# Issuing the column groups of a modulation block together, in a two-layer hybrid diffusion kernel on one core

## The chip, the core and the metric

The kernel runs on one core of a Trainium2 chip. The metric is device time in microseconds of one execution. The engines are called as in the profile: PE multiplies matrices (PEld loads its weights), DVE, ACT and POOL are the vector, scalar and GpSimd engines, SP issues most DMA transfers. Each engine works through its own instructions in order, and they wait for each other through semaphores.

## The reference, cut to what matters

Two layers run over 256 context and 512 latent tokens with 1024 channels. Each layer takes six vectors (shift, scale and gate, twice) from a modulation product:

```
mod_l = silu(c)     @ mod_w[i] + mod_b[i]     # 6144 columns, latent stream
mod_c = silu(c_ctx) @ mod_w[i] + mod_b[i]     # the same weights, context stream
sh1, sc1, g1, sh2, sc2, g2 = split(mod, 6)
p = (norm(x) * (1 + sc1) + sh1) @ w_in[i]     # first modulation: shift, scale
y = concat(gmlp(p), attention(p), deltanet(p))
x = layer_norm(a * x + g1 * (y @ w_out[i]))   # gate
x = layer_norm(a * x + g2 * mlp(norm(x) * (1 + sc2) + sh2))
```

The attention has six query heads on two key and value heads. The DeltaNet is a gated recurrence over chunks of 64 tokens, for six heads, forward and backward.

## The kernel before, in words

**Tiling.** Tokens lie in six tiles of 128 (two of context, four latent). Most products are made in fp32, or with the operands split into a high and a low part.

**The modulation products of layer 0.** The 6144 columns are taken as three products of 2048 columns: 0 (first shift and scale), 1 (first gate and second shift) and 2 (second scale; the second gate is summed elsewhere). The left operand has 32 columns, two of which are used, so a 512-column group of the product fills one quarter of the rows of an output tile: `pm[32*g : 32*g+32]` for group g. The contraction has `KD` = 8 blocks of 128 channels. Product 0 is `mod_in` (line 451), at the kernel's start: two halves, each 8 blocks of two groups. Product 1 is `mod(0, 1, 4, ...)`: 8 blocks of four groups, 32 matmuls. Product 2 is `mod(0, 2, 2, ...)`: 8 blocks of two groups, 16 matmuls. Each matmul has its own weight tile `modw` (128x512 fp32, 256 KB) from DRAM. In `mod` (line 388) there are four such buffers and one bias tile `modb`: four loads go out ahead, then each step waits in the plan for one tile, issues one matmul and one load. At the end DVE adds the bias (`modb<-mm,modb`), PE transposes the result (`mm<-c_ident,modb`), DVE copies shift or scale, and the gate rows go to DRAM (`gates_d<-modb`).

**The stage they run in.** `mods()` (line 856) is one of several streams that run beside each other (line 887): the scans and operands of three DeltaNet head pairs (`scans`, `makes`: rows of the trace with `S`, `vn`, `rr`, `rT`, `rK`, `rQ`, `rW`, `rA`, `gs`), the preparation of the third pair (`prep(2)`: inverses, `PA`, `PB`, `M`), and the attention by tile and head (`akh`, `akl`, `qs`, `ape`, `apT`, `ava`). The pairs 0 and 1 are scanned first, pair 2 after them. A latent attention head is four score matmuls `akh`, `akl`, with the transposes `c_ident,ape` and products `ava,apT` of the head before.

**What sets the order.** The order is made twice. The class `Flow` interleaves the streams while the program is traced: it keeps a rough cost of each instruction (`cost`, line 74) and goes on with the stream whose last step ends first; a stream can give a key or a time that it waits for. `BIAS` and `AHEAD` put some streams ahead. A scheduler then orders each engine's instructions by its own estimate of their times. Instructions that were traced one behind the other may so stand apart.

All instructions are issued by one helper, so every row of the trace has line L206.

**The last piece that the change touches** is `z_gate` (line 1017): the gate of the DeltaNet's output of token tile t, made by `vz` (line 825) after the projections.

Of the kernel before, what the change touches and what calls it, by code (L numbers as in the profile page):

```python
# [39 lines left out]
class Flow:  # L40
    """Interleaves streams of work (generators that yield after each step) as they are traced. The engines run what is
    traced in order, so the stream whose last step ends first, by a rough cost of each instruction, goes on next. A stream
    yields a generator to start it, a key to wait until that key is in `done`, a tuple of classes of PSUM tiles to get,
    or the time to go on."""

    # wait for a result of the same engine, of another one
# [14 lines left out]
    def lend(self, cls, tiles):  # L61
        """PSUM tiles for the streams to ask for"""
        self.spare[cls] = [(0.0, i) for i in range(len(tiles))]
        for i, t in enumerate(tiles):
            self.slots[cls, i] = t
# [8 lines left out]
    def cost(self, eng, op, out, ins, kw):  # L74
        n = max([self.width(out)] + [self.width(a) for a in ins])
        if eng == "tensor":
            n, m = self.width(out), out.shape[0]
            if op == "transpose":
                return 0.87 * n
            if ins[-1].dtype == F32R:  # L80
                return max(35.0 + 0.56 * m, 0.42 * n)
            return 2.0 * max(35.0 + 0.62 * m, 0.83 * n)
# [32 lines left out]
    def when(self, s):  # L115
        """the time a stream can go on, None while what it waits for is not there"""
        t, w = s[0], s[3]
        if isinstance(w, str):
            return max(t, self.done[w]) if w in self.done else None
        if w:  # L120
            for cls in set(w):
                k = w.count(cls)
                if len(self.spare[cls]) < k:
                    return None
                t = max(t, sorted(self.spare[cls])[k - 1][0])
        return t

    def run(self, *gens, side=(), drain=False):
        """until the streams gens end; those of side go on in the next run if they have not ended, or else with drain"""
# [37 lines left out]
    def step(self, gen, val, ahead):  # L167
        """one step of a stream, its instructions as if they were traced that much earlier"""
# [8 lines left out]
    def aside(self, gen):  # L177
        """starts a stream that need not end with the run"""
        self.start(gen, self.last, False)

    def start(self, gen, now, main, bias=0.0, ahead=0):
        """a stream, or a list of it with the ns and the instructions it has ahead of others"""
# [5 lines left out]
    def drop(self, ap):  # L188
        """gives a PSUM tile back, after the last instruction on it"""
# [21 lines left out]
class _Core:  # L211
    """the engines, with a note of all that is issued to them"""
# [6 lines left out]
def _tb(v):  # L219
    """token tile whose chunks the backward direction takes at step pair v (the forward one takes tile v)"""  # L220
# [7 lines left out]
class Feed:  # L228
    """units of weights in order: float32 loaded `raw` ahead, at most `parts` of them as float32r parts, after a
    product with scale(i) where it gives one; the loads start after the key hold"""  # L230
# [53 lines left out]
class K:  # L284
# [22 lines left out]
    def setup(self):  # L307
# [29 lines left out]
        # scratch in DRAM  # L337
# [7 lines left out]
    def store(self, out, in_):  # L345
        """a store, traced when the data is about to be there: loads keep a queue to themselves"""
# [6 lines left out]
    def psum(self, *ns):  # L353
        """PSUM tiles of n columns, to be dropped after their last use"""
# [12 lines left out]
    def feed(self, name, side, srcs, raw, parts, scale=None, hold=""):  # L367
        """a pool for weight units with the stream that loads and splits them"""
# [12 lines left out]
    def rsqrt(self, out, in_, n, scale=1.0, eps=EPS):  # L381
        """out = (in_ * scale + eps) ** -0.5 on [P, n]"""
# [5 lines left out]
    def mod(self, l, j, n, wt, bt, bufs):  # L388
        """the first n groups of 512 columns from column j*2048 of the modulation, both streams; pieces of weights in tiles
        wt(), a bias tile from bt()"""  # L390
# [18 lines left out]
        for i in range(n * KD):  # L409
            k, g, w = i // n, i % n, ws.pop(0)  # L410
            yield flow.ready[w.tensor.name][0]
            nc.tensor.matmul(pm[32 * g : 32 * g + 32], self.cz[:, k, :], w, start=(k == 0), stop=(k == KD - 1))
            if i + bufs < n * KD:
                load(i + bufs)
                if i + bufs == n * KD - 1:
                    flow.signal(f"mw{l}{j}")
# [34 lines left out]
    def mod_in(self, wt, bt, bufs):  # L451
        """shift and scale of the first layer's input, one half of the channels after the other"""
# [52 lines left out]
    def mod_dve(self, l, w, ss, wt, at, vt, bufs):  # L505
        """vector w (shift, scale, gate; twice) of the modulation for the streams ss, summed over the channel blocks on the
        vector engine and over the partitions by the tensor engine"""
# [67 lines left out]
    def norm_act(self, out, x, n):  # L575
        """(x - mean) * rstd on the scalar engine"""
# [6 lines left out]
    def modulate(self, l, which, t, xn, xh, xl, vt, ks=(0, 1), share=False):  # L583
        """normalised token tile t: scaled and shifted, to channel-major parts, in the halves ks of the channels; with share
        the vector engine scales some"""
# [32 lines left out]
    def chan(self, unit, xh, xl, rng):  # L618
        """channel-major block: psum [P, tokens] for the token columns of rng"""
# [14 lines left out]
    def tokm(self, units, rows, w, c0, c1, t, xh, xl):  # L634
        """token-major block: psum [P, c1-c0] for token tile t; units[i] holds the k-rows rows[i], each w wide"""
# [22 lines left out]
# head start of the longest chain over other streams, ns  # L658
BIAS = 1000.0
# instructions the first preparations are ahead for the scheduler  # L660
AHEAD = 300
# units of the hidden layer taken together; more at the end, where the norms follow each tile
# pieces of the first modulation weights loaded ahead
# [3 lines left out]
# channel blocks of each half that the vector engine takes in the first modulation  # L667
# [3 lines left out]
class Kernel(K):  # L671
# [23 lines left out]
    def mix(self, l, xp, xh, xl, rest):  # L695
        """rest: pools of the layer before that its last streams use"""
# [5 lines left out]
        # gMLP: u channel-major, v token-major with the gates of the DeltaNet  # L702
# [75 lines left out]
        # the weights of the next phase come in meanwhile  # L778
# [6 lines left out]
        # DeltaNet: convolutions of all heads, preparation of the first pairs; attention: q, k, v; gate of the DeltaNet  # L785
# [61 lines left out]
        # attention proper beside the scans  # L847
# [94 lines left out]
    def att_tab(self, l, at):  # L942
        """rotary tables times the norm gains: [q|k, cos|sin, tile, channel]"""
# [14 lines left out]
    def qk_norm(self, l, t, h0, ps, at):  # L958
        """rms-norm and rotary of the q|k heads h0.. of token tile t, then channel-major"""
# [57 lines left out]
    def z_gate(self, l, t, ps):  # L1017
        """silu(z) times the gain of the DeltaNet's output norm"""
        nc, ap_ = self.nc, self.atmp
        pz, ps = ps, ps[:, 128:512]  # L1020
        if t == self.tiles[0]:
# [15 lines left out]
    def attention(self, l, at):  # L1037
        """scores of a head run ahead of the products of the head before"""
# [13 lines left out]
        for t in self.tiles:  # L1052
            n = CTX if t < 2 else TOK
            sl = slice(t * P, t * P + P)
            # q as [hi; lo] on the contraction rows, [lo; hi] for odd heads
# [80 lines left out]
    def dn_conv(self, l, u, c0, r, qkv):  # L1136
        """q, k or v of a head pair from its projection r: convolution, silu, norms; token-major"""
# [11 lines left out]
        # outputs run over cb columns a..b  # L1149
# [15 lines left out]
        # acc is twice the silu; to token-major  # L1165
# [11 lines left out]
        else:  # L1177
            # sums of squares over the channels of each head
# [7 lines left out]
            # l2 norm of x = acc / 2 with its guard; q also carries 1/8  # L1186
# [15 lines left out]
    def dn_gates(self, l, gt, gp, dp, G):  # L1202
        """decay sums and rates of all heads, [P, direction, tile, head]"""
# [18 lines left out]
        # softplus(x) = max(x, 0) + log(1 + e^-|x|), the log as 2 atanh(e / (2 + e))  # L1222
# [25 lines left out]
        # running sums of g within a chunk, from the start (gc) and to the end (rem), per direction  # L1248
# [10 lines left out]
        # gc as rows, to be broadcast over partitions through DRAM  # L1259
# [10 lines left out]
        # the rate beta scales columns forward (with k in the state's update), rows backward (with k and v in the solve)  # L1270
# [13 lines left out]
        # decay of a whole chunk on the state's partitions (direction, dk): [ , step pair, e, head]  # L1284
# [13 lines left out]
    # zero quarters of a block-diagonal lhsT [K, v, head, 2 e + column half, 64], by K half  # L1298
# [9 lines left out]
    def a_tiles(self, l, pool, p):  # L1308
        """compact operands of head pair p: products of queries and keys by group, inverses"""
# [16 lines left out]
    def dn_prep(self, l, p, qkv, G, A, TT):  # L1326
        """products of keys and of queries with keys in each chunk of a head pair, and the transposed inverse of the
        unit-triangular system TT [token, (direction, head, tile), token of the chunk]"""
# [19 lines left out]
        # decay between tokens; rows of M hold j forward and i backward  # L1348
# [59 lines left out]
        # inverses of the unit-triangular 32x32 diagonal blocks, one block per partition  # L1408
# [22 lines left out]
        # X[r, c] is the transposed inverse's [c, r]  # L1431
# [6 lines left out]
        # the off-diagonal 32x32 blocks  # L1438
# [33 lines left out]
    def dn_make(self, l, p, v, qkv, G, A, TT, r):  # L1472
        """operands of the two steps of step pair v"""
# [10 lines left out]
        def rows(w, src, sb):  # L1484
            """src scaled by token, forward and backward tiles side by side, to channel-major blocks"""
# [451 lines left out]
```

## Time and profile before

| what | value |
|---|---|
| time, median of three runs | 2101.5 us (2100.75 to 2103.27) |
| profiled execution, span | 2099.3 us |
| what lies around the span (median less span) | 2.2 us |
| mean granted clock of PE | 0.958 |
| PE busy | 1944.5 us, 93% of the span |
| DVE, ACT, POOL busy | 1358.6 (65%), 921.4 (44%), 195.3 us (9%) |
| stage with scans, attention and modulation products of layer 0 | about 302 to 575 us |

The profiled execution has no time of its own beside its span. Most `f32` matmuls have two records in the trace: "x2" is one matmul `mm<-modw,cz` of a product, "x4" are two of them. A row of the time line starts when the instructions do, and idle time in front of it stands in brackets with its releaser. Ends of matmuls are modelled and overlap the next start, so a slot is read from start to start.

### The profile page before, as it was taken

How to read it: one execution, taken by the hardware profiler on the slowest of the kernel's cores; microseconds unless marked ns; L12 is line 12 of the kernel's file. 1: busy time of each engine (PE TensorE's matmuls, PEld its weight loads, DVE VectorE, ACT ScalarE, POOL GpSimd, SP SyncE). 2: the span in 40 equal slices, each digit the busy share in tenths (PEclk: the TensorE clock that was granted, in tenths of full speed). 3: DMA queues.
4: the chain of work that ended last, by engine and by line, in shares of the span. 5: the costliest groups of instructions: out<-in, count | busy, mean ns of one | idle time of the engine just before them, and what ended most of it. 6: DMA issues, size and time to landing. Idle time of an engine off the chain costs nothing. (4 is left out here: it accounts for less than half of the span.)

```text
span 2099.3 us, 31005 instructions
## 1 busy us (share of the span) xinstructions
PE 1944.5 (93%) x11870; PEld 1601.5 (76%) x11870; DVE 1358.6 (65%) x2659; ACT 921.4 (44%) x1881; POOL 195.3 (9%) x375
## 2 busy tenths in 40 slices
PE   6999779989898999999999989997988889999998
PEld 2887655678777888888888778875877768788886
DVE  5578887865577436362457777889896485544555
ACT  4444346566645322322232265443866445422341
POOL 1111221010012000000000111122100010000001
PEclk8999989989999999999999979977999999999999
DMA  7311024312335424241445243110101434322231
GB/s 280 103 46 51 16 75 149 117 40 64 112 110 181 132 72 159 81 140 43 139 161 173 98 142 95 53 36 26 34 23 30 166 129 164 107 90 81 96 107 59
DMA packets 98240, 208.91 MB, mean 100 GB/s; under 512 B 30850, under 2 KB 45058, under 8 KB 98092
## 3 DMA queue, kind: packets, MB, share of 16 engines
q1 hardware_dynamic: 86956, 189.24, 27.9%
q10 hardware_dynamic: 11136, 17.70, 2.2%
q8 instruction: 93, 1.52, 0.3%
q14 instruction: 55, 0.45, 0.1%
HBM read 184.38 MB, written 17.79 MB: 96 GB/s over the span
## 5 line engine op out<-in xcount | busy, mean ns | idle before, releaser
L206 ACT ACTIVATE whi<-wraw 128x1024 fp32r<-128x1024 f32 (+2 forms) x188 | 194.9, 1050 | 440.6 <-PE ax L206 287.8
L206 DVE TENSOR_TENSOR wlo<-wraw,whi 128x1024 fp32r<-128x1024 f32 (+2 forms) x188 | 226.4, 1211 | 224.6 <-ACT whi L206 224.1
L206 PE MATMUL mm<-x2xh,whi 128*128 128x256 f32 (+1 forms) x832 | 288.4, 347 | 10.5 <-ACT whi L206 9.0
L206 PE MATMUL mm<-x2xh,wlo 128*128 128x256 f32 (+1 forms) x832 | 287.3, 346 | 1.6 <-DVE wlo L206 1.6
L206 PE MATMUL mm<-x2xl,whi 128*128 128x256 f32 (+1 forms) x832 | 287.7, 346 | 0.0
L206 PE MATMUL ax<-whi,hh 128*128 128x512 f32 x640 | 251.2, 392 | 0.0
L206 PE MATMUL ax<-whi,hl 128*128 128x512 f32 x640 | 250.0, 391 | 0.0
L206 PE MATMUL ax<-wlo,hh 128*128 128x512 f32 x640 | 249.9, 390 | 0.0
L206 PEld LDWEIGHTS mm<-x2xh,whi 128*128 128x128 f32 x832 | 158.9, 191 | 34.1 <-ACT whi L206 9.4
L206 DVE TENSOR_TENSOR acc<-acc,ax 128x1024 f32<-128x1024 f32 x68 | 82.9, 1219 | 148.3 <-PE ax L206 148.1
L206 PEld LDWEIGHTS mm<-x2xh,wlo 128*128 128x128 f32 x832 | 158.6, 191 | 22.6 <-DVE wlo L206 2.4
L206 PEld LDWEIGHTS mm<-x2xl,whi 128*128 128x128 f32 x832 | 158.8, 191 | 19.9
L206 PEld LDWEIGHTS ax<-whi,hh 128*128 128x128 f32 x640 | 120.2, 188 | 29.7 <-ACT hh L206 5.2
L206 PEld LDWEIGHTS ax<-whi,hl 128*128 128x128 f32 x640 | 120.1, 188 | 27.5 <-DVE hl L206 2.9
L206 PEld LDWEIGHTS ax<-wlo,hh 128*128 128x128 f32 x640 | 120.2, 188 | 27.0 <-issue 2.6
L206 ACT ACTIVATE rl<-mm 128x256 f32<-128x256 f32 (+1 forms) x104 | 50.7, 490 | 129.1 <-PE mm L206 123.7
L206 DVE SCALAR_TENSOR_TENSOR acc<-modw,cz,acc 128x1024 f32<-128x1024 f32 x80 | 101.2, 1280 | 8.4 <-DMA acc<-in_mod_b 5.4
L206 POOL TENSOR_SCALAR rs<-mv 128x1 f32<-128x1 f32 x52 | 33.1, 637 | 699.1 <-DVE mv L206 696.8
L206 PE MATMUL mm<-ava,apT 128*128 128x128 f32 x624 | 88.4, 285 | 2.7 <-ACT apT L206 1.2
L206 PEld LDWEIGHTS mm<-ava,apT 128*128 128x128 f32 x624 | 78.8, 197 | 7.2 <-ACT apT L206 3.2
L206 DVE TENSOR_TENSOR hl<-rl,hh 128x768 fp32r<-128x768 f32 (+2 forms) x76 | 54.4, 716 | 29.4 <-ACT hh L206 29.4
L206 DVE SCALAR_TENSOR_TENSOR cacc<-cb,cw,cacc 128x772 f32<-128x772 f32 (+1 forms) x72 | 69.7, 972 | 0.7 <-ACT cacc L206 0.2
(255 smaller groups left out, 4178.5 us busy)
## 6 DMA issues: line engine op xcount, KB each, us to landing
wraw<-in_w_up SPq DMA_DIRECT2D x64, 512.0 KB
wraw<-in_w_down SPq DMA_DIRECT2D x64, 512.0 KB
modw<-in_mod_w SPq DMA_DIRECT2D x56, 512.0 KB
modw<-in_mod_w SPq DMA_DIRECT2D x80, 256.0 KB
wraw<-in_w_ch SPq DMA_DIRECT2D x22, 512.0 KB
wraw<-in_w_out SPq DMA_DIRECT2D x16, 512.0 KB
x_d<-xt ACTq DMA_DIRECT2D x16, 512.0 KB
xt<-x_d SPq DMA_DIRECT2D x14, 512.0 KB
```

Source lines behind the costliest of these rows:

```text
L206: return f(*args, **kw)
```

## The change

Four pieces, all of them in the code that makes the order:

1. In `mod`, a step takes the tiles of all groups of a block (four in product 1, two in product 2), waits in the plan for the latest of them, issues the block's matmuls one behind the other, and then the same number of loads. A key `mw01`, `mw02` for which nothing waits is gone.
2. `Flow.cost` counts a fp32 product with 32 rows and 512 columns at `0.6 * n` = 307 ns where it counted 850 ns. Product 0 (`mod_in`) consists of such matmuls too.
3. `z_gate` begins with a wait of the plan: for the z gate of the tile before, and for the first tile, for the last tile's queries and keys.
4. Docstrings and comments are gone; the helper's line is L209.

```diff
 def cost(self, eng, op, out, ins, kw):
...
                 return max(35.0 + 0.56 * m, 0.42 * n)
+            if m == 32 and n == 512:
+                return 0.6 * n
             return 2.0 * max(35.0 + 0.62 * m, 0.83 * n)
...
 def mod(self, l, j, n, wt, bt, bufs):
...
         pm = yield from self.psum(512)
-        for i in range(n * KD):
-            k, g, w = i // n, i % n, ws.pop(0)
-            yield flow.ready[w.tensor.name][0]
-            nc.tensor.matmul(pm[32 * g : 32 * g + 32], self.cz[:, k, :], w, start=(k == 0), stop=(k == KD - 1))
-            if i + bufs < n * KD:
-                load(i + bufs)
-                if i + bufs == n * KD - 1:
-                    flow.signal(f"mw{l}{j}")
+        for k in range(KD):
+            part = [ws.pop(0) for _ in range(n)]
+            yield max(flow.ready[w.tensor.name][0] for w in part)
+            for g, w in enumerate(part):
+                nc.tensor.matmul(pm[32 * g : 32 * g + 32], self.cz[:, k, :], w, start=(k == 0), stop=(k == KD - 1))
+            for i in range(k * n + bufs, min((k + 1) * n + bufs, n * KD)):
+                load(i)
             yield
...
 def z_gate(self, l, t, ps):
...
         pz, ps = ps, ps[:, 128:512]
+        yield f"z{l}{t - 1}" if t > self.tiles[0] else f"qk{l}{LT[-1]}"
```

In the compiled order only layer 0 up to the end of the stage differs; POOL's order, the layer's MLP and layer 1 stand as before. Three places are shown.

On PE, in the middle and at the end of product 1. `modw,cz` is a matmul of the product, `c_ident,modb` the transposes of its result, the other names are scans and attention. Before, in the middle:

```order
L206 MATMUL mm_68<-ava,apT 128x128 x2
L206 MATMUL mm_66<-modw,cz 32x512 x2
L206 MATMUL mm_67<-c_ident,gs 128x128 x2
L206 MATMUL mm_69<-rr,rT_2737 128x128 x2
L206 MATMUL mm_66<-modw,cz 32x512
L206 MATMUL mm_68<-S,rQ_2747 128x128 x2
L206 MATMUL mm_67<-c_ident,gs 128x128 x2
L206 MATMUL mm_66<-modw,cz 32x512
```

And now, at the end of product 1 and the first matmul of product 2:

```order
L209 MATMUL mm_69<-modw,cz 32x512
L209 MATMUL mm_66<-S,rQ_2749 128x128 x2
L209 MATMUL mm_66<-vn,rA_2754 128x128 x2
L209 MATMUL mm_68<-S,rQ_2697 128x128 x2
L209 MATMUL mm_69<-modw,cz 32x512 x2
L209 MATMUL mm_66<-S,rW_2682 128x128
L209 MATMUL mm_69<-modw,cz 32x512
L209 MATMUL mm_66<-S,rW_2682 128x128
L209 MATMUL mm_69<-modw,cz 32x512
L209 MATMUL mm_69<-c_ident,modb 128x128 x4
L209 MATMUL mm_67<-rr,rT_2713 128x128 x2
L209 MATMUL mm_69<-modw,cz 32x512
```

A block of four stands as two, one and one, with other matmuls between, and the transposes stand directly behind the last matmul of product 1, where 13 rows stood between them before. The pairs of product 2 stand two to five rows of other matmuls apart. In the whole stage the 48 matmuls of products 1 and 2 stood in 36 groups of neighbours (24 and 12) and stand in 32 (23 and 9).

On PE, at the inverse of the third pair, whose first matmuls `PB,M` wait for DVE. `ape` and `apT` are parts of an attention head, `akh` and `akl` its scores. Before:

```order
L206 MATMUL ax_71<-PB,M 32x32 x26
L206 MATMUL mm_68<-S,rQ_2721 128x128 x2
L206 MATMUL mm_68<-vn,rA_2726 128x128 x2
L206 MATMUL ax_71<-PB,M 32x32 x9
L206 MATMUL mm_69<-c_ident,gs 128x128 x2
L206 MATMUL ax_71<-PB,M 32x32 x13
L206 MATMUL mm_66<-c_ident,modb 128x128 x4
L206 MATMUL mm_68<-S,rW_2706 128x128 x2
```

And now:

```order
L209 MATMUL ax_70<-PB,M 32x32 x12
L209 MATMUL mm_68<-vn,rA_2780 128x128 x2
L209 MATMUL ax_70<-PB,M 32x32 x24
L209 MATMUL mm_66<-c_ident,ape 128x128 x2
L209 MATMUL ax_70<-PB,M 32x32 x12
L209 MATMUL mm_67<-ava,apT 128x128 x3
L209 MATMUL ax_71<-akh,qs 128x512
L209 MATMUL ax_71<-akl,qs 128x512
```

Scans of the first two pairs and the transposes of product 2 stood beside this inverse; now attention heads do, and the products are over before. When the last of the 36 scan steps is issued, 12 of the latent heads are out where 9 were, so 12 stand behind it where 15 stood.

On DVE, at the start: `v` and `xl` belong to the modulation of a token tile's channel half, `modb<-mm,modb` is the bias of product 0's second half, `sh` and `sc` its shift and scale. Before:

```order
L206 TENSOR_SCALAR v<-mm_69,sc_0_98,sh_0_97 128x128 x2
L206 TENSOR_TENSOR xl<-v,xh 128x4x128 x2
L206 TENSOR_SCALAR v<-mm_66,sc_0_98,sh_0_97 128x128 x2
L206 TENSOR_SCALAR v<-mm_69,sc_0_98,sh_0_97 128x128 x2
L206 TENSOR_TENSOR xl<-v,xh 128x4x128 x2
L206 TENSOR_TENSOR modb<-mm_68,modb 64x512
```

And now:

```order
L209 TENSOR_SCALAR v<-mm_69,sc_0_98,sh_0_97 128x128 x2
L209 TENSOR_TENSOR xl<-v,xh 128x4x128
L209 TENSOR_TENSOR modb<-mm_68,modb 64x512
L209 TENSOR_SCALAR sh_0_97<-mm_67 128x8
L209 TENSOR_SCALAR sc_0_98<-mm_67 128x8
L209 TENSOR_SCALAR v<-mm_68,sc_0_98,sh_0_97 128x128 x2
```

Six tiles' first halves stood before the bias, three do now, and three moved behind it.

On SP, the loads of weight tiles stood singly or in twos among other transfers; now they stand mostly in fours (product 1) and twos (product 2). At the change from product 1 to product 2 stands:

```order
L209 DMA modw<-in_mod_w 128x512
L209 DMA gates_d<-modb 1x512 x4
L209 DMA modw<-in_mod_w 128x512 x3
L209 DMA modb<-in_mod_b 2x512 x2
L209 DMA rT_2687<-TT_1019 64x2x64 x2
```

Three of product 2's first four weight tiles are loaded behind the four stores of the gate, which read the biased result of product 1.

## Rows read from the trace of the kernel before

**Rows 1.** The page: span, and busy time of PE.
```profile
span 2099.3 us, 31005 instructions
...
PE 1944.5 (93%) x11870; PEld 1601.5 (76%) x11870; DVE 1358.6 (65%) x2659; ACT 921.4 (44%) x1881; POOL 195.3 (9%) x375
```

**Rows 2.** Busy time of engines by stretch, granted clock (PEclk), DMA share.
```profile
core 0: us, PE busy (x) PEld busy (x) DVE busy (x) ACT busy (x) POOL busy (x), PEclk, DMA share, GB/s
312.00:420.00 108.00, 105.48 (x718) 64.67 (x717) 83.98 (x299) 65.61 (x208) 11.11 (x50) 0.98 0.44 135
420.00:456.00 36.00, 32.53 (x364) 28.16 (x364) 25.42 (x88) 22.17 (x75) 2.82 (x3) 0.81 0.12 31
456.00:520.00 64.00, 59.74 (x456) 54.79 (x455) 40.05 (x138) 43.69 (x151) 2.48 (x2) 0.97 0.17 49
520.00:570.00 50.00, 45.16 (x348) 41.35 (x349) 27.43 (x68) 33.28 (x77) 2.47 (x2) 1.00 0.42 137
432.00:444.00 12.00, 12.00 (x168) 10.47 (x162) 6.44 (x28) 8.19 (x30) 0.00 (x0) 0.57 0.01 3
```

**Rows 3.** Time line of PE at products 1 and 2: start, us.
```profile
316.69 1.04 PE L206 MATMUL mm<-modw,cz 128*32 128x512 f32 x2
317.67 0.39 PE L206 MATMUL ax<-akh,qs 128*128 128x256 f32 x1
...
319.60 1.05 PE L206 MATMUL mm<-modw,cz 128*32 128x512 f32 x4
320.58 0.44 PE L206 MATMUL mm<-c_ident,gs 128*128 128x128 f32 x2
...
373.37 1.06 PE L206 MATMUL mm<-modw,cz 128*32 128x512 f32 x6
374.36 0.71 PE L206 MATMUL mm<-rr,rT 128*128 128x128 f32 x4
```

**Rows 4.** Time line of PE in product 0: twelve records without a change.
```profile
34.50 2.77 PE L206 MATMUL mm<-modw,cz 128*32 128x512 f32 x12
37.20 0.66 PE L206 MATMUL mm<-c_ident,xt 128*128 128x128 f32 x4
```

**Rows 5.** PE's transposes of a product's result: at the start, in the stage.
```profile
20.52 0.66 PE L206 MATMUL mm<-c_ident,modb 128*128 128x128 f32 x4 [0.83 <-DVE modb L206]
...
380.60 0.49 PE L206 MATMUL mm<-c_ident,modb 128*128 128x128 f32 x3
```

**Rows 6.** Issue of the first weight loads, and the first matmul that waits.
```profile
3.83 1.30 SPq L206 DMA_DIRECT2D modw<-in_mod_w  x3
...
6.86 1.89 PE L206 MATMUL mm<-modw,cz 128*32 128x512 f32 x2 [6.86 <-DMA modw<-in_mod_w]
```

**Rows 7.** Waits from 302 to 660 us: total us, times, longest.
```profile
PEld mm L206 <- DMA modw<-in_mod_w: 1.8, 2, 1.1
```

**Rows 8.** Time line of PE at the inverse of the third pair.
```profile
431.56 1.01 PE L206 MATMUL ax<-PB,M 32*32 32x32 f32 x52 [1.76 <-DVE PB L206]
```

**Rows 9.** Time line of PE in the tail: scores of one head, of the next.
```profile
562.68 0.48 PE L206 MATMUL ax<-akh,qs 128*128 128x512 f32 x1
...
565.45 0.48 PE L206 MATMUL ax<-akh,qs 128*128 128x512 f32 x1
```

**Rows 10.** Time line of DVE at the start, around the second bias.
```profile
34.85 1.43 DVE L206 TENSOR_SCALAR v<-mm,sc,sh 128x128 f32<-128x128 f32 x4 [0.33 <-ACT v L206]
36.34 1.39 DVE L206 TENSOR_TENSOR xl<-v,xh 128x512 fp32r<-128x512 f32 x2
...
42.88 0.17 DVE L206 TENSOR_SCALAR sh<-mm 128x8 f32<-128x8 f32 x1 [0.81 <-PE mm L206]
...
46.02 0.69 DVE L206 TENSOR_TENSOR xl<-v,xh 128x512 fp32r<-128x512 f32 x1 [1.50 <-ACT xh L206]
```

## The prediction, made before the changed kernel ran

> **What bounds the kernel now.** I read the page first: PE is busy for 1944.5 of a span of 2099.3 us [rows 1], so work taken off PE can count wherever PE is full. Next, busy time by stretch, because an average says nothing on the stage in question. In 312 to 420 us, where nearly all matmuls of products 1 and 2 run, PE is busy for 105.48 of 108 us at a clock of 0.98 [rows 2]: PE is the bound there. In the two stretches behind it PE has 3.5 and 4.3 us free, and in the tail, 520 to 570 us, 4.8 [rows 2]. The granted clock falls only around the third pair's inverse: 0.57 over 432 to 444 us, after PE had stood idle for 1.76 us behind DVE's `PB` [rows 2, 8]. 0.57 lies between the two levels of 1.2 and 2.4 GHz, so these 12 us lose 12 x (1 - 0.57) = 5.2 us against full clock.
>
> Then the time line of PE at the products. A single matmul of 32 columns takes 317.67 - 316.69 = 0.98 us from start to start, two neighbours 0.98, three 0.99 [rows 3]. So groups that stand next to each other already run side by side, and what counts is the number of bursts, not of matmuls. Last, the waits: PE waited for weight tiles twice in the stage, 1.8 us in all [rows 7].
>
> **The change, part by part.**
>
> *a) Bursts.* The code wants 8 bursts of four and 8 of two, 16. The order gives 32 where 36 stood: the scheduler takes the blocks of four apart. Four bursts fewer at 0.98 us [rows 3] are -3.9 us. PE is full there, so I count all of it; where a burst went out of a place in which PE then waits for the chains of the scans anyway, it is 0. Range -3.9 to 0. Each product keeps its 48 matmuls, and the bursts that stay take what they took.
>
> The Trainium skill (TensorEngine Tiling (Array Packing), Key Properties) says that a change of the tiling mode drains the engine, and one could take that drain for all that a burst less gives back. Six matmuls without a change take 2.70 us, three pairs at 0.90 [rows 4], so a change costs at most 0.08 us, and four fewer would be 0.3 us instead of 3.9. Rows 3 decide: a third matmul in a burst is free, so the burst itself goes.
>
> *b) The change of products.* The transposes now follow the last matmul of product 1 directly on PE and need DVE's bias first. At the start, where they also follow directly, that wait was 0.83 us, and in the stage before, with 13 rows between, none [rows 5]. Three of product 2's first four loads stand on SP behind the gate's stores, which need the same bias; from issue of a first load to the matmul that needs it pass 6.86 - 3.83 = 3.03 us [rows 6]. The first tile was loaded ahead of the stores, and scan matmuls stand in front of the second. So 0 to +3.0, and below nothing is excluded, since nothing gets shorter here. I take +0.9, near the row of the transposes. Also behind the waiting loads on SP are transfers of `rT` for later scan pairs; they have the time of a whole scan step.
>
> *c) Loads of a block.* In product 1 each load still waits for the matmul of its own buffer alone, and SP issues it in that order, so the turn of a buffer stays what it was: 0, and one wait like the 1.1 us in rows 7 if the gap is short. In product 2 a pair's two buffers come back two pairs later. With g of other matmuls in each gap, a load has 0.98 + 2g, and wants 3.03 [rows 3, 6]. With g = 0 each of the three rounds lacks 2.05 us, together +6.1; with g over 1.0 us nothing is lost. The order shows two to five rows of scan matmuls in most gaps, which puts g about at that point. I take +1.0, below the 1.8 us that the trace of before has for such waits in all [rows 7]. Nothing gets shorter, so the lower end is 0.
>
> The Trainium skill (DMA: Bandwidth & Descriptors, Anatomy of one DMA — SWDGE (gpsimd) path) has a fixed 2.0 us and the bytes at 436 GB/s for one transfer. An estimate from that is 2.6 us for 256 KB, less than the 3.03 us from row to row, which hold the issue too. With 2.6 us the point from which nothing is lost would fall to g = 0.8 us and this term to about 0; the row is what I use.
>
> *d) The start.* The lower cost also moves product 0. On DVE three first halves (`v` two pairs 1.43/2, `xl` 1.39/2, together 1.41 us each [rows 10]) now stand behind the second half's bias where they stood ahead. If all of it were new on the path, +4.2 us. Against it: the bias itself comes earlier by that, and DVE idled for 0.81 and 1.50 us just behind it [rows 10], into which 2.3 us of the moved work fits. So -2.3 (the idle goes and nothing else is late) to +4.2. I take +1.0, half of what is left over, 4.2 - 2.3 = 1.9; what is late next is the input of the first projections, which PE takes tile by tile.
>
> *e) The tail.* Three latent heads move out of the tail, up to the place beside the third pair's inverse. In the tail a head takes 565.45 - 562.68 = 2.77 us [rows 9], so up to -8.3 leaves the tail; but PE has to run them elsewhere. Free of charge is only what PE idles beside the inverse, 1.76 us, and the 5.2 us that the clock costs there if the added matmuls keep it up [rows 2, 8]: -6.9 at most. At the least 0: work moved from one full stretch to another. I take -3.0, the idle time and about a quarter of the clock's loss, because the stall behind `PB` stays DVE's and DVE too has attention work moved ahead of `PB`. The wait in `z_gate` moves its operations by about one place each: 0, behind the projections that hold PE.
>
> *Sum.* -3.9 + 0.9 + 1.0 + 1.0 - 3.0 = -4.0 us on a span of 2099.3, so 2095.3. The span lies 2.2 us under the median of the timed runs, which I add again: **2097.5 us**. About 0.2%, 4.2 us, is what a measurement of this kernel tells from no change; the forecast lies right at that bound.
>
> **Rivals.**
>
> *The change doesn't do what it says.* The blocks stand apart as 2, 1 and 1, and what four fewer bursts give goes into the loads: -3.9 + 0.9 + 2.7 for c (half way to its upper end, less what covers it), and nothing from the tail or the start: -0.3, 2101.2 us. For it: the order with 32 bursts. Against it: PE waited for these loads only for 1.8 us before [rows 7].
>
> *Slower.* The products are filler: PE has work from them while scans wait for DVE. They are gone earlier now, and the stretch from there to the inverse holds chains alone. The place is the one behind the last matmul of product 2. If PE idles there for as long as once before `PB`, 1.76 us, and the clock then falls for 12 us as it did, 5.2 us more are lost [rows 2, 8]: +7.0 on top of -3.9 + 0.9 + 1.0 + 1.0 with nothing from the tail, +6.0, 2107.5 us. It decides from an idle time of that length on. For it: the only low clock of the stage follows just such an idle time. Against it: three heads have been moved into that stretch.
>
> *Much faster.* The three heads fill the inverse's idle time and keep the clock: -6.9 instead of -3.0, and b to d are covered: -3.9 - 6.9 = -10.8, 2090.7 us. If all blocks ran whole, 16 bursts, it would be -19.6 from the bursts alone, 2081.9 us; the order speaks against that, as every burst on PE is a row there.
>
> **How the numbers follow.** Forecast 0.50, no effect 0.19, slower 0.18, much faster 0.13. The forecast's own range is 2092 to 2103, from half the distance to the bounds of its terms. The range that holds 8 in 10 leaves out the lower part of the much faster case and the upper half of the slower one: 2088 to 2107. Faster than 2097.3: about 0.55 of the forecast, a tenth of no effect and all of much faster, 0.42. Slower than 2105.7: 0.15 of the slower rival, 0.05 of the others' upper ends, 0.20. Within: 0.38.
>
> **What would show it.** (a) The time line of PE at the products has 32 bursts of about 0.98 us, whatever their size; a burst of four that takes twice as long would make a) wrong. (b) Idle time before the transposes and before the next `modw` matmul, 0.9 us in all; 3 us would show the stores in the way. (c) Waits of PE for `modw` of about 2 to 3 us in the stage. (d) The first projections start within 1 us of before. (e) The clock from the inverse on above 0.57, and the stage's last scan nearer to its end. If the stage from 302 us to the first output product is not shorter by about 5 us and the rest unchanged to a microsecond, the sum is wrong, even where the total fits.

## The result and the profile after

| | before | changed |
|---|---|---|
| median | 2101.1 us (2099.3 to 2103.3) | 2121.6 us (2116.9 to 2122.0, 4 runs) |
| profiled span | 2099.3 us | 2114.6 us |

The ratio is 1.0096, interval 1.0081 to 1.011: the change makes the kernel slower by 20 us, against a forecast of 4 us faster and a range up to 2107. The profiled execution of the changed kernel is the fastest of its four runs, 2116.9 us. The trace therefore shows 15.3 of the 20.5 us; the other 5 are a spread between runs that no profile of this kernel covers. The ratios, here and below, are not quotients of the medians; the two differ by up to 0.0015 (in cost_only below), which is 3 us.

The page of the changed kernel [rows 1 before]:

```profile
span 2114.6 us, 31017 instructions
...
PE 1939.1 (92%) x11870; PEld 1595.3 (75%) x11870; DVE 1357.5 (64%) x2659; ACT 920.5 (44%) x1881; POOL 194.7 (9%) x375
```

PE has 5.4 us less work in a span that is 15.3 us longer, so the loss is idle time, 20.7 us of it. To place it, take four landmarks: the last matmuls of the input projections, where the stage begins, the first `PB,M` matmul of the third pair's inverse, the start of the last scan step, and the first output product behind it (`whi,yh`), where the stage ends. Busy time by these stretches, before (columns as in rows 2):

```profile
301.70:431.60 129.90, 118.30 (x888) 74.67 (x888) 100.17 (x343) 80.41 (x246) 17.97 (x89) 0.96 0.40 123
431.60:512.60 81.00, 75.47 (x692) 68.48 (x693) 51.55 (x181) 55.47 (x187) 5.09 (x4) 0.89 0.15 41
512.60:575.90 63.30, 55.82 (x428) 50.61 (x426) 31.64 (x81) 39.93 (x98) 2.47 (x2) 1.00 0.38 126
```

And of the changed kernel:

```profile
307.00:462.20 155.20, 132.12 (x1005) 89.36 (x1003) 112.56 (x384) 90.57 (x290) 20.45 (x91) 0.97 0.35 109
462.20:533.50 71.30, 63.02 (x634) 56.65 (x634) 43.68 (x150) 50.73 (x154) 2.48 (x2) 0.95 0.17 48
533.50:592.10 58.60, 49.93 (x367) 44.96 (x367) 26.24 (x71) 34.25 (x86) 2.47 (x2) 0.97 0.34 117
```

The stage begins 5.3 us later (307.0 against 301.7) and is 10.9 us longer (285.1 against 274.2); behind it the changed kernel is 0.9 us quicker. In the stage PE is busy for 245.1 us instead of 249.6 and idle for 40.0 instead of 24.6. Of these 15.4 us more, 11.5 lie in the stretch up to the inverse, which became 25.3 us longer (idle 23.1 of 155.2 against 11.6 of 129.9). The two stretches behind it are shorter together, by 14.4 us, as work has moved ahead of the inverse. The clock is not the cause: in the stretch up to the inverse it is 0.97 (0.96 before), and around the inverse's old place it is now full [rows 2 before].

```profile
440.00:480.00 40.00, 27.98 (x355) 23.19 (x355) 29.85 (x95) 25.06 (x86) 4.96 (x4) 0.95 0.11 31
432.00:444.00 12.00, 11.83 (x96) 11.13 (x96) 10.98 (x45) 7.10 (x25) 0.20 (x1) 1.00 0.04 8
```

In 440 to 480 us PE runs for 28.0 of 40 us only. Up to the inverse at 462.18 us it stands idle in many short waits for DVE and ACT, the longest 1.72 us before `PB,M`. Behind the inverse it waits once for 5.03 us, for DVE's `zg` (the gated output of a finished pair), and the granted clock then falls, to 0.66 in 474 to 480 us:

```profile
476.35 1.54 PE L209 MATMUL ax<-c_ident,zg 128*128 128x128 f32 x6 [5.03 <-DVE zg L209]
...
474.00:480.00 6.00, 2.72 (x9) 2.12 (x10) 1.92 (x2) 3.43 (x9) 0.31 (x1) 0.66 0.14 34
```

Time line of PE, the changed kernel [rows 3, 5, 8 before]:

```profile
324.97 1.05 PE L209 MATMUL mm<-modw,cz 128*32 128x512 f32 x4
325.96 0.71 PE L209 MATMUL mm<-rr,rT 128*128 128x128 f32 x4
...
370.84 0.66 PE L209 MATMUL mm<-c_ident,modb 128*128 128x128 f32 x4 [0.84 <-DVE modb L209]
...
388.00 1.65 PE L209 MATMUL mm<-modw,cz 128*32 128x512 f32 x4 [0.37 <-DMA modw<-in_mod_w]
...
400.77 0.68 PE L209 MATMUL ax<-kq 64*64 64x128 f32 x16
...
462.18 0.57 PE L209 MATMUL ax<-PB,M 32*32 32x32 f32 x24 [1.72 <-DVE PB L209]
```

Bursts of one or two without a wait cost 0.98 to 0.99 us as before. The row to look at is `kq`: these are the last key products of the third pair's preparation, from which its triangular solve and inverse follow. Before, they ran at 378.35 us:

```profile
378.35 0.66 PE L206 MATMUL ax<-kq 64*64 64x128 f32 x10
```

and the inverse 53 us later, at 431.56. Now they run at 400.77 and the inverse 61 us later. On PE 32 of the 48 matmuls of products 1 and 2 stood ahead of them; now all 48 do. So the inverse is 30.6 us late: 5.3 us from the start, 17.1 us more up to the key products, and 8.2 us more between these and the inverse. In that last piece lies the solve, on DVE, which runs 207 instructions in this time instead of 170, so more of other streams beside it (columns as in rows 2, before, then now):

```profile
378.35:431.56 53.21, 50.08 (x339) 36.10 (x338) 46.19 (x170) 30.06 (x97) 1.77 (x4) 1.00 0.30 92
400.77:462.18 61.41, 53.61 (x423) 48.06 (x423) 56.77 (x207) 39.58 (x140) 2.68 (x3) 1.00 0.14 36
```

No run here shows whether that work makes the solve longer.

The start, DVE's bias and ACT behind it, before:

```profile
41.38 0.68 DVE L206 TENSOR_TENSOR modb<-mm,modb 64x512 f32<-64x512 f32 x1 [0.47 <-DMA wraw<-in_w_ta]
44.31 1.15 ACT L206 ACTIVATE v<-mm,sh,sc 128x128 f32<-128x128 f32 x3 [4.13 <-DVE v L206]
```

DVE and then ACT of the changed kernel [rows 10 before]:

```profile
37.39 0.69 DVE L209 TENSOR_TENSOR xl<-v,xh 128x512 fp32r<-128x512 f32 x1 [0.76 <-ACT xh L209]
41.24 0.68 DVE L209 TENSOR_TENSOR modb<-mm,modb 64x512 f32<-64x512 f32 x1 [3.16 <-PE mm L209]
```
```profile
43.17 1.16 ACT L209 ACTIVATE v<-mm,sh,sc 128x128 f32<-128x128 f32 x3 [5.82 <-PE mm L209]
```

DVE idles for 3.16 us in front of the bias (0.47 before) and ACT for 5.82 around it (4.13 before). The three halves that stood there before come behind it, while the bias itself comes at 41.24 us where it came at 41.38.

### The profile page after: what moved, and what is told of

Same layout as the page of the kernel before. It is cut to its first block, busy times and chain, and to the rows that moved or that the text cites. A ratio compares the mean times of both kernels' runs of the same rounds, so it can differ in the third digit from the quotient of the medians.

```text
span 2114.6 us, 31017 instructions
## 1 busy us (share of the span) xinstructions
PE 1939.1 (92%) x11870; PEld 1595.3 (75%) x11870; DVE 1357.5 (64%) x2659; ACT 920.5 (44%) x1881; POOL 194.7 (9%) x375
## 4 chain that ended last, share of the span: by engine, by line
PE 65%; DVE 17%; ACT 6%; issue 5%; POOL 4%; DMA 2%; SPq 0%; POOLq 0%; DVEq 0%; ACTq 0%
PE mm L209 41%; PE ax L209 24%; DVE tm L209 2%; DVE Xx L209 2%; POOL crn L209 2%; DVE cacc L209 1%; DVE wlo L209 1%; DVE st L209 1%; POOL rs L209 1%; DVE axn L209 1%; DVE A L209 1%; ACT ape L209 1%; POOL arn L209 1%; DVE M L209 1%; POOL rstd L209 1%
## 5 line engine op out<-in xcount | busy, mean ns | idle before, releaser
L209 ACT ACTIVATE whi<-wraw 128x1024 fp32r<-128x1024 f32 (+2 forms) x188 | 194.5, 1050 | 436.6 <-PE ax L209 287.6
L209 DVE TENSOR_TENSOR wlo<-wraw,whi 128x1024 fp32r<-128x1024 f32 (+2 forms) x188 | 226.4, 1211 | 226.4 <-ACT whi L209 225.7
L209 PE MATMUL mm<-x2xh,whi 128*128 128x256 f32 (+1 forms) x832 | 288.3, 347 | 10.5 <-ACT whi L209 8.9
L209 PE MATMUL mm<-x2xh,wlo 128*128 128x256 f32 (+1 forms) x832 | 287.1, 345 | 1.1 <-DVE wlo L209 1.1
L209 PE MATMUL mm<-x2xl,whi 128*128 128x256 f32 (+1 forms) x832 | 287.6, 346 | 0.0
L209 PE MATMUL ax<-whi,hh 128*128 128x512 f32 x640 | 251.2, 393 | 0.0
L209 PE MATMUL ax<-wlo,hh 128*128 128x512 f32 x640 | 250.1, 391 | 0.0
L209 PE MATMUL ax<-whi,hl 128*128 128x512 f32 x640 | 250.0, 391 | 0.0
L209 PEld LDWEIGHTS mm<-x2xh,whi 128*128 128x128 f32 x832 | 158.9, 191 | 34.0 <-ACT whi L209 9.4
L209 DVE TENSOR_TENSOR acc<-acc,ax 128x1024 f32<-128x1024 f32 x68 | 82.9, 1219 | 147.3 <-PE ax L209 147.1
L209 PEld LDWEIGHTS mm<-x2xh,wlo 128*128 128x128 f32 x832 | 158.5, 191 | 22.1 <-DVE wlo L209 1.9
L209 PEld LDWEIGHTS mm<-x2xl,whi 128*128 128x128 f32 x832 | 158.7, 191 | 20.0
L209 PEld LDWEIGHTS ax<-whi,hh 128*128 128x128 f32 x640 | 120.2, 188 | 29.8 <-ACT hh L209 5.2
L209 PEld LDWEIGHTS ax<-whi,hl 128*128 128x128 f32 x640 | 120.1, 188 | 27.5 <-DVE hl L209 2.9
L209 PEld LDWEIGHTS ax<-wlo,hh 128*128 128x128 f32 x640 | 120.2, 188 | 27.3 <-issue 2.6
L209 ACT ACTIVATE rl<-mm 128x256 f32<-128x256 f32 (+1 forms) x104 | 50.7, 489 | 129.9 <-PE mm L209 125.0
L209 DVE SCALAR_TENSOR_TENSOR acc<-modw,cz,acc 128x1024 f32<-128x1024 f32 x80 | 101.1, 1281 | 7.9 <-DMA acc<-in_mod_b 5.7
L209 POOL TENSOR_SCALAR rs<-mv 128x1 f32<-128x1 f32 x52 | 32.4, 623 | 700.5 <-DVE mv L209 699.3
L209 PE MATMUL mm<-ava,apT 128*128 128x128 f32 x624 | 89.7, 286 | 2.7 <-ACT apT L209 1.7
L209 PEld LDWEIGHTS mm<-ava,apT 128*128 128x128 f32 x624 | 79.6, 198 | 7.9 <-ACT apT L209 4.4
L209 DVE TENSOR_TENSOR hl<-rl,hh 128x768 fp32r<-128x768 f32 (+2 forms) x76 | 54.5, 717 | 29.3 <-ACT hh L209 29.3
L209 ACT ACTIVATE v<-mm,sh,sc 128x128 f32<-128x128 f32 x152 | 58.3, 466 | 28.9 <-PE mm L209 25.4
```

What stands on the lines that cost most here:

```text
L209: return f(*args, **kw)
```

## The experiments

The medians of the kernel before beside these runs were 2100.4 to 2100.9 us.

**The start undone (start_back).** The lower cost counts in `mod` alone:

```diff
-            if m == 32 and n == 512:
+            if m == 32 and n == 512 and self.cheap:   # set around the matmuls in mod
                 return 0.6 * n
```

> The changed kernel, with the lower cost counted only in the second and third product; the first product's order at the start is that of before, the stage's order that of the change. Theory: the start costs 5.4 us of its own (first convolution at 119.7 instead of 114.3 us, and that offset stays to 307 us) and the stage 11 to 15 us apart from it. Then the first convolution comes at 114.3 us again and the time falls by 5 to 6 us, to about 2116. Rival: the late start is swallowed by the stage, which has idle time; then the time stays within 2 us of 2121.6.

Measured: 2112.2 us (2109.6 to 2117.9), ratio 1.006 [1.0047, 1.0072], a larger gain than expected. The first convolution is back at 114.2 us and the stage's start at 301.5; the inverse stays late, 458.7 us. The start is a cause by itself: 5.3 us in the traces, some 8 by the ratios. The stage stays long: 291.5 us in this trace, which is that of the slowest of the five runs.

```profile
397.35 0.68 PE L209 MATMUL ax<-kq 64*64 64x128 f32 x16
...
458.69 0.57 PE L209 MATMUL ax<-PB,M 32*32 32x32 f32 x24 [1.66 <-DVE PB L209]
...
593.01 1.22 PE L209 MATMUL mm<-whi,yh 128*128 128x512 f32 x2 [2.10 <-ACT whi L209]
```

**The third pair's `DB` loads off SP (after_db).** `DB` holds the decay sums that the third pair's preparation needs. In the changed kernel its two loads stand on SP behind 24 and 28 weight loads, where they stood behind 16 and 18, and were issued at 351.6 and 358.1 us instead of 334.0 and 337.8. My first theory was that this delays the third pair.

```diff
-            nc.sync.dma_start(
+            (nc.scalar if l == 0 and p == 2 else nc.sync).dma_start(
                 out=DB[_half(hf)]...
```

> The changed kernel, with the two loads of DB for the third pair's preparation in layer 0 issued from ACT's queue instead of SP's; the weight loads stay where they are. Theory: the stage is longer because these loads stand on SP behind 24 and 28 weight loads instead of 16 and 18, each of which waits for a matmul of a product, so that the third inverse's first matmul comes at 462 instead of 432 us. Then DB is issued near 315 to 330 us, the inverse comes at about 435 to 445 us, and the time falls by 8 to 12 us, to 2110 to 2114. Rival: the inverse is late because DVE's and PE's own order puts scans and attention ahead of it; then it stays later than 455 us and the time within 3 us of 2121.6.

Measured: 2121.9 us, ratio 1.0102 [1.0088, 1.0115], no change. ACT issues the loads early, and DVE takes them up 26 us earlier than in the changed kernel (364.39), but what follows does not move (ACT's queue, DVE, PE):

```profile
330.40 0.51 ACTq L208 DMA_DIRECT2D DB<-gc_d  x1
...
338.76 0.95 DVE L208 TENSOR_TENSOR DB<-DB,gc 128x768 f32<-128x768 f32 x1
...
401.89 0.68 PE L208 MATMUL ax<-kq 64*64 64x128 f32 x16
...
463.27 0.57 PE L208 MATMUL ax<-PB,M 32*32 32x32 f32 x24 [0.64 <-DVE PB L208]
```

That theory fell. The same edit in the other two kernels agrees:

> The kernel before, with the two loads of DB on ACT's queue. Theory (the queue of SP sets the third preparation): DB comes some 10 us earlier than at 334 and 338 us, the inverse 5 to 10 us earlier than at 432 us, and the time falls by 0 to 5 us, to 2096 to 2101. Rival (DVE's order sets it): no change within 1 us.

Measured: 2102.2 us, ratio 1.0005 [0.9996, 1.0014], no change.

> The changed kernel with both: the start's order of before, and the DB loads on ACT's queue. Theory: the two causes add up, so that what is left is the change's gain of the bursts and of the tail, 2098 to 2108 us. If the stage is longer for another reason, 2113 us or more.

Measured: 2114.6 us, ratio 1.0068 [1.0055, 1.0081], as start_back alone; the inverse at 457.5 us. So something behind `DB` holds the third pair: the last key products.

**Product 2 held back (hold2).** start_back, and in the plan product 2 waits for the third pair's key products:

```diff
 def dn_prep(...):            # behind the three groups of key products
+        if l == 0 and p == 2:
+            self.flow.signal("gram2")
 def mods():
             yield from self.mod(0, 1, 4, wt, bt, 4)
+            yield "gram2"
             yield from self.mod(0, 2, 2, wt, bt, 4)
```

> The kernel start_back, in which the third product waits in the plan until the three groups of key products of the third pair's preparation are traced. Theory: the third pair is the long chain, and the change puts all 48 matmuls of the products ahead of its last key products on PE where 32 stood before; 9 bursts of about 0.98 us and the waits at the change of products delay it. With 32 again, the last key products come at 378 to 388 us instead of 397, the third inverse's first matmul at 435 to 448 instead of 459, the first output product by 580 to 586 instead of 593, and the time is 2100 to 2106. Rival: the products' place does not matter, the inverse is late because DVE's steps are interleaved with more scans; then the inverse stays later than 455 us and the time at 2112 or more.

Measured: 2105.3 us (2102.3 to 2109.6), ratio 1.0015 [1.0006, 1.0024]. PE:

```profile
375.08 0.68 PE L209 MATMUL ax<-kq 64*64 64x128 f32 x16
...
435.81 0.95 PE L209 MATMUL ax<-PB,M 32*32 32x32 f32 x48 [0.46 <-DVE PB L209]
...
575.15 1.22 PE L209 MATMUL mm<-whi,yh 128*128 128x512 f32 x2 [2.08 <-ACT whi L209]
```

The key products come 22 us and the inverse 23 us earlier than in start_back, the first output product 18 us (593.0 to 575.2). Part of these 18 us is the choice of runs: start_back's traced run is the slowest of five, hold2's one of the faster of eleven. By the medians the two kernels lie 7 us apart, by the ratios 9. The place of product 2 is a cause of the late third pair, and with it back most of the stage's loss is gone.

**The mirror (push).** The kernel before, in which the third pair's last key products wait for product 2:

```diff
 def dn_prep(...):            # in the loop over the groups g of key products
+            if l == 0 and p == 2 and g == 2:
+                yield "mod02"
             ps = yield from self.psum(512)
```

> The kernel before, with one wait of the plan added: the last group of key products of the third pair's preparation waits for the end of the third product. The mirror of hold2: 48 matmuls of the products ahead of these key products instead of 32, nothing else of the change. 10 heads then stand ahead of the inverse on PE instead of none. Theory: a late third pair makes the stage long, by as much as PE finds no other work; the last key products come after 420 us instead of 378, the inverse after 465, and the time rises by 4 to 15 us, to 2105 to 2116. Rival: the third pair's place makes no difference to the time and hold2 gained by something else; then within 2 us of before.

Measured: 2129.4 us, ratio 1.0137 [1.0124, 1.0151], more than expected.

```profile
441.18 1.15 PE L206 MATMUL ax<-kq 64*64 64x128 f32 x16
...
495.36 2.77 PE L206 MATMUL ax<-PB,M 32*32 32x32 f32 x96 [4.08 <-DVE PB L206]
...
598.98 0.73 PE L206 MATMUL mm<-whi,yh 128*128 128x512 f32 x2 [2.35 <-ACT whi L206]
```

An inverse that is 64 us late puts the first output product 23 us back, with nothing else of the change. The span is 28 us longer; the other 5 lie behind the output product and are not explained. The wait put the key products far behind, so this is a larger dose than in the changed kernel: it shows the direction, not its size there.

**The loop and the z gate's wait without the lower cost (no_cost), the lower cost alone (cost_only).** The diff of the change without the lower cost, and with nothing else.

> The changed kernel without the lower cost: the loop by blocks and the wait in the z gate alone. All 48 matmuls of the products still stand ahead of the third pair's last key products, in 28 bursts. Theory: the loop alone makes the stage long, and the lower cost only the start; the time is that of start_back within 3 us, 2109 to 2116. Rival: the lower cost, which makes the plan take the products for cheap, makes the stage long; then 2099 to 2104.

Measured: 2106.1 us, ratio 1.0021 [1.0011, 1.003]: neither the theory nor the rival. The key products (397.9 us) and the inverse (459.7) are as late as in start_back, so the lower cost is not needed to put product 2 ahead of them. But the first output product comes at 582.7 us instead of 593.0. With the old cost 4 latent heads stand ahead of the inverse instead of 2, and only 11 are left behind the last scan instead of 12. PE from the last scan to the first output product, no_cost:

```profile
534.10:582.70 48.60, 42.33 (x309) 37.92 (x307) 22.77 (x60) 28.95 (x76) 2.47 (x2) 0.96 0.42 142
```

48.6 us, where the changed kernel has 58.6; 7.6 of these 10.0 us are PE's work, nearly all of it attention that no_cost does earlier. The reading that fits is that a late third pair costs less where attention work fills the wait ahead of the scans' end, and that the lower cost takes such work away from there. No run moves the attention heads alone.

> The kernel before with the lower cost alone, in all three products. The start is the one of the change, and 28 matmuls of the products stand ahead of the third pair's last key products. Theory: the start costs 5 to 8 us and the stage nothing, so 2105 to 2109. Rival: the lower cost makes the stage long too; 2115 or more.

Measured: 2110.1 us, ratio 1.0029 [1.0019, 1.0039]. First convolution at 118.8 us, stage from 306.2 to 579.5 us, 273.3 long against 274.2. The lower cost alone spoils the start and not the stage: 28 matmuls of the products stand ahead of the third pair's last key products there, not 48. Behind the stage this trace is 3.3 us longer than that of before, which is not explained.

**Without the wait in the z gate (no_z).**

```diff
-        yield f"z{l}{t - 1}" if t > self.tiles[0] else f"qk{l}{LT[-1]}"
```

> The changed kernel without the wait in the z gate. The start is that of the change, 48 matmuls of the products stand ahead of the last key products, and 3 heads ahead of the inverse instead of 2, 11 behind the last scan instead of 12. Theory: the wait costs nothing where it stands, but the stage's order that the plan draws is another; late third pair as in the change, first convolution at 119 us, time 2112 to 2122. Rival: the wait itself is a cause of the loss; 2107 or less.

Measured: 2113.6 us, ratio 1.0059 [1.0046, 1.0072]. Late start (119.8 us) and late inverse (464.5) as in the change, first output product at 585.2 instead of 592.1; again fewer heads are left, 11 instead of 12. The wait changes the plan's order and through it some 8 us of the time, by the medians of both kernels. I had put it at 0. The two traces are only 1.0 us apart, because the part behind the output product takes 1528.3 us here and 1522.5 in the changed kernel; why is not known. The third pair is late here without the wait, in no_cost without the lower cost, and not in cost_only: what the late ones share is the loop. The loop alone, with nothing held back, was not run.

**Attempts at a better version.** All products held back (hold_all), the loop alone with product 2 held (loop_hold2), and the loop alone with its stream 1000 ns behind in the plan (bl1000: `[mods(), -1000.0]`).

> The kernel start_back, in which both products wait until the third pair's key products are traced. None of the 48 matmuls stands ahead of the last of these, 44 stand ahead of the inverse. Theory: the long chain gets PE first and the products fill the time in which PE waits for the solve on DVE; the inverse comes before 430 us and the time is below that of before, 2085 to 2098. Rival: scans and attention hold up the third pair anyway, and filler is missing at the stage's start: 2100 to 2108.

Measured: 2107.1 us, ratio 1.0025 [1.0015, 1.0036]. The key products come at 361 us, 17 earlier than before, and the inverse still at 435: the piece between them grew from 53 to 74 us, with the products now beside the solve. That these make the solve slow is the likely reading; it was not tested by itself.

> The loop by blocks alone (old cost, no wait in the z gate), with the third product held back until the third pair's key products are traced. 33 bursts, the third pair where it was in the kernel before. Theory: what is left of the change is the saving of three to four bursts (3 us) less the waits for loads; the inverse's first matmul at 428 to 436 us and the time 2097 to 2102. Rival: the loads of whole blocks cost more than the bursts give back; 2104 or more.

Measured: 2110.7 us, ratio 1.0053 [1.004, 1.0066], the rival's side. The inverse is early (436.3 us), but PE's waits for weight tiles are these, for weights and for matmuls [rows 7 before: 1.8]:

```profile
PEld mm L206 <- DMA modw<-in_mod_w: 6.8, 7, 1.7
...
PE mm L206 <- DMA modw<-in_mod_w: 2.6, 4, 0.8
```

Whether these waits make the whole loss was not tested.

> The loop by blocks alone, with the products' stream put 1000 ns behind the others in the plan, as the scans and the third preparation are put ahead. 32 bursts, 32 matmuls of the products ahead of the third pair's last key products, 13 heads behind the last scan instead of 16. Theory: products that give way to the third pair everywhere keep it early and leave filler for the inverse; inverse before 436 us, time 2093 to 2101. Rival: as hold_all, the chain gets slower by the filler that moves beside its solve: 2103 to 2108.

Measured: 2105.6 us, ratio 1.0024 [1.0015, 1.0034]; inverse at 434.0 us, first output product at 578.7 instead of 575.9. None of the versions beats the kernel before.

## Why the prediction was wrong, point by point

- *a) Bursts*, -3.9 us: right on PE's own time: 32 bursts instead of 36. From start to start they sum to 34.6 us in the trace of the changed kernel and to 38.2 before, -3.6. This sum holds more than the count: the first three matmuls of product 1 last 2.02 instead of 4.02 us, and the waits of b and c are in it.
- *b) Change of products*, +0.9: right, 0.84 us before the transposes of product 1. The stores were not in the way.
- *c) Loads of a block*, +1.0: right for product 2. Three of its pairs took 1.02 to 1.58 us instead of 0.98, 0.8 us more together, and one of them began 0.37 us late. That nothing gets shorter was wrong: the 1.8 us of before, at the start of product 1, are gone, so that PE's weight loads waited for tiles for 1.0 us in the stage in all. In another arrangement of the same loop they waited 6.8 us (loop_hold2): 5.0 more than before, near my upper end of 6.1.
- *d) The start*, +1.0: mis-sized, 5.3 us, above the upper end of 4.2. The step that failed was the cover, "the bias itself comes earlier by that". The bias waits for PE's last matmul of product 0, and came 0.14 us earlier. So the moved halves did not fill idle time; they left it: 3.16 us on DVE, where there had been 0.47. My sign for this term, first projections that start within 1 us of before, came true (47.53 us against 47.18) and did not show the loss: the projections behind the first ones wait, and PE is busy for 10.6 us in 44 to 60 us where it was for 13.4.
- *e) The tail*, -3.0: wrong sign, and the main error; this is the step that failed in the stage. I priced the heads that left the tail and the idle time beside the inverse, and took the inverse's own time as given. It is not: it hangs on the third pair's key products, and the change put product 2 ahead of them. The stage, which a, b, c and e together made 5.0 us shorter, grew by 10.9 us in the trace. The cover I named, heads beside the inverse, did move there, and the clock was 1.00 in 462 to 474 us, but the inverse came 30.6 us later. I also read that the clock falls only around the inverse; in the kernel before it is 0.50 in 311.5 to 315.5 us too, after 4.61 us of idle time.
- PE's busy time in the stage did fall, by 4.5 us, and bought nothing. "PE is full there, so I count all of it" was read from one stretch, while the stage's end is set by the third pair, which PE reaches later.
- *The slower rival* had the right side and half the mechanism: filler gone too early, PE idle up to the inverse. Its price, 7 us with a fall of the clock, was that of one stall; what happened was 11.5 us more idle time, of many waits, at a clock of 0.97 up to the inverse; the clock fell only behind it, to 0.66 over 474 to 480 us. The rival was given 0.18.
- *The z gate*, 0: wrong as a term of the plan: the changed kernel is some 8 us slower with it than without (no_z).

Shown: the start by start_back and cost_only; that the place of product 2 is a cause by hold2 and, in direction, by push; that it is not the whole by no_cost, which keeps product 2 ahead and is still 6 us faster than start_back. Argued, not shown: that the heads decide how much a late pair costs, since in no_cost and no_z they move with the rest of the order. Refuted: the `DB` loads. Open: the 8.2 us between key products and inverse; the 5 us by which the profiled run lies under the median of its kernel; the part behind the first output product, up to 6 us longer in some of these kernels; and whether the time of product 2's bursts on PE or only the plan's later issue of the key products holds those back, since every edit here moves both.

## What to carry to other kernels

Where a planner sets the order, look for what moved in front of the longest chain, and count it at the chain's own steps: 48 instead of 32 matmuls ahead of one row of PE told more than the busy share of the stretch. A new estimate in the plan moves what stands beside the estimated work, even where nothing runs faster: the lower cost made no matmul faster and cost the start 5 us, while the kernels with product 2 ahead of the third pair share the loop. And a saving on a full engine counts only if that engine, and not a chain through it, ends the stage.

## What the runs showed of the hardware

One or two 32-column matmuls side by side take the same 0.98 to 0.99 us in a burst, in the kernel before and after; three took 0.99 us in the kernel before [rows 3]. At a granted clock of 0.50, the lower level of 1.2 GHz (319.0 to 321.5 us of the changed kernel, behind 5.04 us of idle time) three took 2.02 us. A block of four that stayed whole (no_cost) took 2.20 us, as the fourth weight tile came late; its price without a wait was not seen.

```profile
359.97 2.20 PE L206 MATMUL mm<-modw,cz 128*32 128x512 f32 x8
```
```profile
361.13 0.14 PEld L206 LDWEIGHTS mm<-modw,cz 128*32 128x32 f32 x2 [1.01 <-DMA modw<-in_mod_w]
```
